# First pair of gate/up blocks: plain products by halves of tokens instead of Strassen's seven, with the sums for later blocks made meanwhile on VectorE

## The chip, the cores and the metric

The kernel runs on one core of a Trainium2 chip. That core has five engines with a queue of instructions each: TensorE (PE, matrix products, with the loading of its stationary operand shown apart as PEld), VectorE (DVE), ScalarE (ACT), GpSimd (POOL) and SyncE (SP, which here issues DMA transfers). They run side by side and wait for one another through semaphores. The metric is the device time of one execution in microseconds. A profile of one execution shows every instruction with start and duration.

## What is computed

One layer of a hybrid network on 640 tokens (512 latent tokens and 128 context tokens) of 2048 features: modulation, a mixing part (a recurrent scan beside a gated unit), an output projection with a residual, and a channel mixer. The part that matters here is the last two steps, from the reference:

```python
    x = x + g1 * (jnp.concatenate([o_a, o_b], axis=-1) @ lp['w_out'])
    h = _rmsnorm(x, lp['norm2_g']) * (1.0 + sc2) + sh2
    ff = (jax.nn.silu(h @ lp['w_ffn_gate']) * (h @ lp['w_ffn_up'])) @ lp['w_ffn_down']
    return x + g2 * ff, s_fin
```

The hidden width of the channel mixer is 5632, that is 44 blocks of 128 columns. Everything is float32.

## The kernel before

**Precision.** TensorE multiplies in a reduced float32 format (`F32R`). Each operand is therefore split into a high part (a cast, on ACT) and a low part (the operand less its high part, on DVE), and a product is the sum of three matmuls: hi x hi, hi x lo, lo x hi. `operand` (L1249) splits a 128x320 piece of the activations, `parts` (L1349) a 128x512 tile of weights (four 128x128 stationary operands). A tile of weights is loaded by one DMA of 256 KB, cast on ACT (L1352), subtracted on DVE (L1353) and used by 12 matmuls of 320 columns.

**Strassen.** The activations stand transposed in 16 tiles `x1T[0..15]` of 128 features x 640 tokens. The tokens fall into two halves, `t1` and `t2`, of 320; the features into two halves of eight tiles (`x1T[j]` and `x1T[j + 8]`). A gate block and the up block of the same columns form the other factor, again two halves of features by two of outputs. A product of 2x2 blocks takes eight block products, or seven in Strassen's way (the Winograd form) with sums on both sides. `seven` (L1408) does one block in seven products in the order `PORD` = 1, 2, 3, 7, 5, 6, 4, each of 24 matmuls: 168 matmuls a block. The sums of the weights are made by `combined` on POOL (L1366), 8 instructions a block. The operands of the activations, `X[i, j]` for product i and feature tile j, are made once and stay in memory for all 44 blocks: 1 and 2 are the plain first token half, 5 starts from the sum of the two feature halves of the second token half, 6, 3 and 7 from differences, 4 is plain.

**The seam.** The output projection (L1295 to L1315) runs in two passes, first for `t1`, then for `t2`, over 16 column tiles. After each pass the sum of squares over the features is complete (`stats`, L1285), and the scale `rs` for that half of the tokens comes from DVE, ACT and DVE (L1291 to L1293). For `t1` the normalized activations (`first_half`) are made during the second pass, and so are operands 1 and 2 for j below 4. Those of `t2` can only begin when the second pass and its statistics are done. `second_half(j)` (L1326) then scales two tiles (one on DVE, one on POOL), applies the modulation on ACT in two pieces, makes Strassen's sums partly on POOL (L1339, L1344), partly on DVE (L1340, L1342), and splits the operands.

`seven_first` (L1368) computes block 0 with all seven products open at once: half of products 1 and 2, then `second_half` for j = 0 to 3, then the first half of the features of the other products, with `second_half` for j = 4 to 7 between them, then the rest.

**What sets the order.** Each engine runs its queue strictly in order. The order within a queue is fixed when the kernel is built: the framework goes by the order in the program, takes the earliest instruction that its own time model says is ready, and adds the waits. A tile can be allocated when the tile that had its tag before is no longer read. What the model has wrong shows on the chip as an engine waiting at the head of its queue with other work behind.

**Later.** A `Gate` object takes the seven sums of a block from the matmul accumulators, forms gate and up, applies SiLU and multiplies (`act`). After each pair of blocks `stores` makes the Strassen sums of `act` for the down projection on POOL and writes them to memory (`d_op`, `d_os`). The down projection (L1733) works in the same way; `load_ops` (L1460) fetches its operands during the last gate/up block into tiles whose tags `stags` lists (then L1481 and L1482 split them), and `load_down` (L1447) its weights into tiles whose tags `wtags` lists. Those tags are places of `x1T`, which hold operands of the gate/up blocks until these end. `ops` and `dloads` are advanced at set products of the last block.

## Time and profile before

| | us |
|---|---|
| median of three runs | 3535.55 |
| lowest and highest | 3533.24, 3540.5 |
| the profiled execution | 3527.76 |
| its span, first to last instruction | 3526.0 |

Busy time in the span: PE 3283.1 us (93%), weight loads 2943.3 (83%), DVE 2523.4 (72%), ACT 1438.5 (41%), POOL 1269.8 (36%). The mean granted clock of TensorE is 0.961 of full speed.

How to read the rows: a row of the timeline gives start and duration in us, engine, line of the kernel, operation, output tile, input tiles and shape; "x2" means that two instructions are merged into the row; in brackets stands how long the engine had been idle and what ended it ("<-ACT hi L1352": the cast of line 1352 on ACT). A row of groups gives the busy time and the mean duration in ns of one instruction, then the idle time before them. A row of stretches gives the busy time of each engine in that stretch, the granted clock, the busy share of the DMA engines, and GB/s. A row "who waited for whom" gives the total wait, how often, and the longest.

### The profile page before, as it was taken

Reading aid. Unit: us, or ns where it says so; the run is one execution under the profiler, and the core shown is the slowest. Engines: PE = TensorE matmul, PEld = TensorE weight load, DVE = VectorE, ACT = ScalarE, POOL = GpSimd, SP = SyncE. Lnnn points to the kernel's source line nnn. Section 1 sums busy time; section 2 is a strip of 40 time slices with the busy share of each in tenths; the row PEclk is TensorE's granted clock in tenths of the full one; section 3 lists DMA queues with packets and bytes.
Section 4 is the critical chain, followed back from the end, with each engine's and each line's share of the span. In section 5 each row is a group of like instructions: output and inputs, shape, how many; then the busy total and the mean of one; then the engine's idle time right before and its main releaser. Section 6 shows DMA issues by size and latency. Waiting matters only on the chain.

```text
span 3526.0 us, 72626 instructions
## 1 busy us (share of the span) xinstructions
PE 3283.1 (93%) x28212; PEld 2943.3 (83%) x28212; DVE 2523.4 (72%) x4524; ACT 1438.5 (41%) x3123; POOL 1269.8 (36%) x1066
## 2 busy tenths in 40 slices
PE   6999989998899999999769999999999999999996
PEld 3687767776777877778769999999999999999986
DVE  4547557756766766654788788888888877877787
ACT  3333334433443433333454444444444444443355
POOL 0001111111111103230356565656565644555533
PEclk8998999998999999998879999999999999999998
DMA  8666666656666767644423434343434345544553
GB/s 315 231 196 169 169 167 181 187 163 154 175 173 174 182 203 230 207 148 137 143 60 111 127 107 123 111 126 107 124 111 125 106 152 162 167 128 123 156 168 111
DMA packets 728049, 546.97 MB, mean 155 GB/s; under 512 B 139496, under 2 KB 661752, under 8 KB 718872
## 3 DMA queue, kind: packets, MB, share of 16 engines
q1 hardware_dynamic: 717176, 528.63, 50.1%
q0 software_dynamic: 8192, 13.13, 2.0%
q8 instruction: 222, 3.64, 0.4%
q14 instruction: 123, 1.01, 0.1%
q10 hardware_dynamic: 2336, 0.57, 0.1%
HBM read 433.53 MB, written 111.28 MB: 155 GB/s over the span
## 4 chain that ended last, share of the span: by engine, by line
PE 39%; DVE 6%; issue 5%; DMA 3%; ACT 1%; POOL 1%; DVEq 0%; SPq 0%; ACTq 0%; POOLq 0%
PE P L1431 13%; PE P L1429 12%; PE P L1430 12%; DVE lo L1353 2%; DMA d_os<-act 2%; DVE act L1554 1%; DMA opd<-d_op 1%; DVE xo L1256 0%; DVE xd L1482 0%; PE big L1306 0%; PE big L1304 0%; PE big L1305 0%; ACT hi L1352 0%; DVE out L1788 0%; POOL rawd L1366 0%
## 5 line engine op out<-in xcount | busy, mean ns | idle before, releaser
L1431 PE MATMUL P<-xo,lo 128*128 128x320 f32 x2408 | 748.5, 311 | 11.4 <-DVE lo L1353 11.4
L1429 PE MATMUL P<-xo,hi 128*128 128x320 f32 x2408 | 746.0, 310 | 2.0 <-ACT hi L1352 1.9
L1430 PE MATMUL P<-xo,hi 128*128 128x320 f32 x2408 | 744.7, 309 | 0.0
L1353 DVE TENSOR_TENSOR lo<-raw,hi 128x512 fp32r<-128x512 f32 x528 | 582.6, 1121 | 72.4 <-ACT hi L1352 67.6
L1352 ACT CAST hi<-raw 128x512 fp32r<-128x512 f32 x528 | 324.5, 622 | 421.7 <-PE P L1430 323.6
L181 PE MATMUL big<-h_hi,hi 128*128 128x320 f32 x1376 | 458.8, 334 | 11.1 <-ACT hi L161 5.5
L1431 PEld LDWEIGHTS P<-xo,lo 128*128 128x128 f32 x2408 | 452.6, 188 | 19.4 <-DVE lo L1353 19.4
L1429 PEld LDWEIGHTS P<-xo,hi 128*128 128x128 f32 x2408 | 452.6, 188 | 4.4 <-ACT hi L1352 4.0
L1430 PEld LDWEIGHTS P<-xo,hi 128*128 128x128 f32 x2408 | 452.7, 188 | 0.0
L183 PE MATMUL big<-h_hi,lo 128*128 128x320 f32 x1376 | 442.7, 323 | 7.6 <-DVE lo L162 7.6
L182 PE MATMUL big<-h_lo,hi 128*128 128x320 f32 x1376 | 443.8, 323 | 0.7 <-DVE h_lo L337 0.7
L1366 POOL TENSOR_TENSOR raw<-raw 128x512 f32<-128x512 f32 x264 | 426.2, 1623 | 16.2 <-DVE lo L1353 5.9
L1431 PE MATMUL P<-xd,lo 128*128 128x320 f32 x1232 | 385.0, 312 | 15.8 <-DVE lo L1353 15.5
L1429 PE MATMUL P<-xd,hi 128*128 128x320 f32 x1232 | 383.0, 311 | 4.6 <-ACT P L1729 2.5
L1430 PE MATMUL P<-xd,hi 128*128 128x320 f32 x1232 | 382.0, 310 | 0.0
L162 DVE TENSOR_TENSOR lo<-raw,hi 128x512 fp32r<-128x512 f32 x268 | 184.9, 694 | 231.2 <-ACT hi L161 219.6
L181 PEld LDWEIGHTS big<-h_hi,hi 128*128 128x128 f32 x1376 | 268.1, 195 | 93.0 <-issue 59.0
L161 ACT CAST hi<-raw 128x512 fp32r<-128x512 f32 x268 | 165.8, 620 | 354.0 <-PE big L182 164.0
L183 PEld LDWEIGHTS big<-h_hi,lo 128*128 128x128 f32 x1376 | 268.0, 195 | 22.0 <-DVE lo L162 10.3
L182 PEld LDWEIGHTS big<-h_lo,hi 128*128 128x128 f32 x1376 | 268.7, 195 | 13.3 <-issue 7.3
L1352 ACT CAST hi<-rawd 128x512 fp32r<-128x512 f32 (+1 forms) x288 | 169.5, 589 | 241.9 <-PE P L1430 206.2
L1431 PEld LDWEIGHTS P<-xd,lo 128*128 128x128 f32 x1232 | 232.5, 189 | 23.0 <-DVE lo L1353 22.8
(358 smaller groups left out, 6287.1 us busy)
## 6 DMA issues: line engine op xcount, KB each, us to landing
wt<-in_w_mod_dram SPq DMA_DIRECT2D x96, 1024.0 KB
rec<-d_S SPq DMA_DIRECT2D x80, 576.0 KB
raw<-in_w_ffn_gate_dram SPq DMA_DIRECT2D x176, 256.0 KB
raw<-in_w_ffn_up_dram SPq DMA_DIRECT2D x176, 256.0 KB
raw<-in_w_in_dram SPq DMA_DIRECT2D x172, 256.0 KB
rawd<-in_w_ffn_down_dram SPq DMA_DIRECT2D x128, 256.0 KB
raw<-in_w_out_dram SPq DMA_DIRECT2D x96, 256.0 KB
xd<-d_os SPq DMA_DIRECT2D x66, 320.0 KB
```

The source lines that it names most:

```text
L161: S.copy(hi, raw)
L162: V.tensor_sub(lo, raw, hi.bitcast(F32))
L181: TE.matmul(halves[hf], hi[:, k, :], h_hi[:, kb, s], start=(kb == 0), stop=False)
L182: TE.matmul(halves[hf], hi[:, k, :], h_lo[:, kb, s], start=False, stop=False)
L183: TE.matmul(halves[hf], lo[:, k, :], h_hi[:, kb, s], start=False, stop=(kb == KB - 1))
L1352: S.copy(hi[:, 0:nk], raw[:, 0:nk])
L1353: V.tensor_sub(lo[:, 0:nk], raw[:, 0:nk], hi[:, 0:nk].bitcast(F32))
L1366: G.tensor_tensor(out=o[:, 0:nk], in0=p[:, 0:nk], in1=q[:, 0:nk], op=ALU.subtract)
L1429: TE.matmul(ps, hi[:, k, :], xk[:, 0, :], start=f, stop=False)
L1430: TE.matmul(ps, hi[:, k, :], xk[:, 1, :], start=False, stop=False)
L1431: TE.matmul(ps, lo[:, k, :], xk[:, 0, :], start=False, stop=l)
L1554: V.tensor_sub(lo, src, hi.bitcast(F32))
```

## The change

Blocks 0 and 1 (f = 0 and its partner, which together form the first pair) are computed by plain products, eight instead of seven per block, and by halves of the tokens. `PLAIN` lists seven entries (block, half of the features, halves of the tokens); an entry takes four tiles of weights. The first four entries need the first token half, the fourth both, the last three the second half alone. The plain operands of the second token half, `X[5, j]` and `X[4, j]`, are made in `second_half`; `sums(j)`, between the later entries, makes Strassen's operands 7, 6 and 3 on DVE, and operand 5 is split a second time at the end, from the sum. `plain_out` forms SiLU(gate) x up from the accumulators. Three tiles of weights are loaded during the last column of the projection, and two of them are split before its last statistic.

```diff
+    JORD = (6, 7, 0, 1, 2, 3, 4, 5)
+    SPARE = ["rs2"] + [f"x1_{m}" for m in (15, 0, 8, 1, 9, 2, 10, 3, 11, 4, 12)]
+
     def operand(i, j, src):
-        if j >= 6 and i != 4:
-            x = xap.tile([P, 2, HALF], F32R, tag=f"x1_{(1, 2, 3, 7, 5, 6).index(i) + 8 * (j - 6)}", name="xo")
+        m = JORD.index(j)
+        if i in (3, 6, 7) and m >= 4:
+            x = xap.tile([P, 2, HALF], F32R, tag=SPARE[3 * (m - 4) + (3, 7, 6).index(i)], name="xo")
         else:
-            x = xpool(i, j).tile([P, 2, HALF], F32R, tag=f"xo{i}_{j}", name="xo")
+            k = m if i in (3, 6, 7) else j
+            x = xpool(i, k).tile([P, 2, HALF], F32R, tag=f"xo{i}_{k}", name="xo")
...
+    PLAIN = ((0, 0, (0,)), (1, 0, (0,)), (0, 1, (0,)), (1, 1, (0, 1)), (0, 1, (1,)), (0, 0, (1,)), (1, 0, (1,)))
+    PW, READY, gus = [], [], []
+    def load_plain():
+        for n, q, _ in PLAIN:
+            for w, k0 in ((w_ffn_gate, 0), (w_ffn_gate, 8), (w_ffn_up, 0), (w_ffn_up, 8)):
+                pool, bufs = (gus[0], RAWB) if gus else (st, 3)
+                raw = pool.tile([P, 4, P], F32, tag="raw", name="raw", bufs=bufs)
+                f, r0 = ORDER[n], (k0 + 4 * q) * P
+                nc.sync.dma_start(raw, w[0, r0:r0 + 512, f * P:f * P + P].rearrange("(k p) n -> p k n", p=P))
+                PW.append(raw)
+                yield
+    first = load_plain()
...
+                if hf and m == KB - 1:
+                    for _ in range(3):
+                        next(first)
                 if sqs:
                     stats()
...
+        for _ in range(2):
+            READY.append(parts(PW.pop(0)))
         stats()
...
     def second_half(j):
-        for kb in (j, j + 8):
+        for kb, i in ((j, 5), (j + 8, 4)):
             x = x1T[kb]
-            (V if kb < 8 else G).tensor_tensor(out=x[:, t2], in0=x[:, t2], in1=rs[:, t2], op=ALU.mult)
+            V.tensor_tensor(out=x[:, t2], in0=x[:, t2], in1=rs[:, t2], op=ALU.mult)
             for (lo, hi, v) in ((HALF, 384, 1), (384, T, 0)):
                 S.activation(x[:, lo:hi], x[:, lo:hi], AF.Identity, scale=modc[4][:, kb, v:v + 1],
                              bias=modc[3][:, kb, v:v + 1])
+            operand(i, j, x[:, t2])
+    def sums(j):
         a11, a21, a12, a22 = x1T[j][:, t1], x1T[j][:, t2], x1T[j + 8][:, t1], x1T[j + 8][:, t2]
-        if j > 3:
-            operand(1, j, a11)
-            operand(2, j, a12)
         s3 = gu.tile([P, HALF], F32, tag="s3", name="s3")
-        G.tensor_tensor(out=s3, in0=a11, in1=a21, op=ALU.subtract)
+        V.tensor_sub(s3, a11, a21)
+        operand(7, j, s3)
         V.tensor_add(a21, a21, a22)
-        operand(5, j, a21)
         V.tensor_sub(a11, a21, a11)
         operand(6, j, a11)
-        G.tensor_tensor(out=a12, in0=a12, in1=a11, op=ALU.subtract)
-        operand(7, j, s3)
-        operand(4, j, a22)
+        V.tensor_sub(a12, a12, a11)
         operand(3, j, a12)
...
-    def seven_first(b11, b12, b21, b22, hook):
...
+    def plain(e):
+        n, q, hs = PLAIN[e]
+        for u in range(2):
+            for b in range(2):
+                hi, lo = READY.pop(0) if READY else parts(PW.pop(0))
+                next(loads, None)
+                for h in hs:
+                    if (n, u, h) not in CP:
+                        CP[n, u, h] = pP.tile([P, 512], F32, tag="P", name="C")[:, 0:HALF]
+                    ps, i = CP[n, u, h], ((1, 2), (5, 4))[h][b]
+                    for k in range(4):
+                        xk = X[i, 4 * q + k]
+                        m = DONE.get((n, u, h), 0)
+                        DONE[n, u, h] = m + 3
+                        TE.matmul(ps, hi[:, k, :], xk[:, 0, :], start=m == 0, stop=False)
+                        TE.matmul(ps, hi[:, k, :], xk[:, 1, :], start=False, stop=False)
+                        TE.matmul(ps, lo[:, k, :], xk[:, 0, :], start=False, stop=m == 45)
+    def plain_out(n, h):
+        if h == 0:
+            acts.append(xap.tile([P, T], F32, tag=f"x1_{6 + n}", name="act"))
+        pa, dst = tmp("pa"), acts[n][:, (t1, t2)[h]]
+        S.activation(pa, CP[n, 0, h], AF.Silu)
+        V.tensor_mul(dst, pa, CP[n, 1, h])
+        if h == 0:
+            nc.sync.dma_start(d_op[0, n], dst)
+    def first_blocks():
+        plain(0)
+        plain(1)
+        for j in range(4, 8):
+            operand(1, j, x1T[j][:, t1])
+            operand(2, j, x1T[j + 8][:, t1])
+        for j in range(4, 8):
+            second_half(j)
+        plain(2)
+        plain(3)
+        for j in range(4):
+            second_half(j)
+        for j in JORD[:2]:
+            sums(j)
+        for n in range(2):
+            plain_out(n, 0)
+        plain(4)
+        plain(5)
+        for j in JORD[2:4]:
+            sums(j)
+        plain(6)
+        for j in JORD[4:]:
+            sums(j)
+        for n in range(2):
+            plain_out(n, 1)
+        for j in JORD:
+            operand(5, j, x1T[j][:, t2])
+        stores(0)
...
-    wtags, stags, ctags = tags(2, 10, 3, 11, 4, 12, 5, 13, 14, 15), tags(0, 8, 1, 9), tags(6, 7, 0, 8)
+    wtags, stags, ctags = tags(13, 2, 11, 10, 4, 3, 12, 5, 14, 15), tags(8, 1, 0, 9), tags(6, 7, 0, 8)
...
-    loads = load_w(0)
-    for _ in loads:
-        pass
-    loads = load_w(1)
-    for _ in range(4):
+    loads = itertools.chain(first, load_w(2), load_w(3))
+    for _ in range(9):
         next(loads)
...
-                self.c = xap.tile([P, 2, HALF], F32, tag=f"x1_{14 + f % 2}", name="c")
+                self.c = xap.tile([P, 2, HALF], F32, tag=f"x1_{(14, 5)[f % 2]}", name="c")
...
-    for f in range(NFF):
+    first_blocks()
+    for f in range(2, NFF):
         b = {n: [WB.pop((f, n, q)) for q in range(2)] for n in ("11", "12", "21", "22")}
         bs = b["11"], b["12"], b["21"], b["22"]
-        for o in seven(*bs, lambda i, k: X[i, k], Gate(f)) if f else seven_first(*bs, Gate(f)):
+        for o in seven(*bs, lambda i, k: X[i, k], Gate(f)):
```

More of the change, by code (lines that the diff above doesn't have):

```diff
@@ L1322, in flow_step @@
     gu = gux.enter_context(tc.tile_pool(name="gu", bufs=2))
+    gus.append(gu)
     xcp = xcx.enter_context(tc.tile_pool(name="xcp", bufs=1, side="right"))
@@ L1366, in combined @@
             G.tensor_tensor(out=o[:, 0:nk], in0=p[:, 0:nk], in1=q[:, 0:nk], op=ALU.subtract)
[L1368 to L1385 removed]
+    CP, DONE = {}, {}
```

43 lines of the change are left out of this document (7 added, 36 removed).

## The prediction

> **What bounds the kernel now.** I read the page first, then the busy table by stretches, to find where TensorE (PE) is not full.
>
> ```profile
> span 3526.0 us, 72626 instructions
> ```
> ```profile
> core 0: us, PE busy (x) PEld busy (x) DVE busy (x) ACT busy (x) POOL busy (x), PEclk, DMA share, GB/s
> ...
> 1742.30:1806.80 64.50, 21.82 (x78) 17.04 (x77) 53.88 (x78) 36.62 (x87) 40.27 (x34) 0.63 0.24 68
> 1822.57:1847.20 24.63, 24.63 (x170) 24.63 (x169) 21.29 (x25) 11.27 (x18) 13.89 (x9) 1.00 0.33 98
> ```
>
> Over the span PE is 93% busy, and the second row (gate/up block 1) shows it full at full clock. The first row is the seam between the output projection and the gate/up blocks: 64.5 us, PE busy in a third of it and at 0.63 of its clock, VectorE (DVE) busy in 53.9 us. The end of the projection in DVE's timeline, PE's timeline after it, and PE's waits from 1742 to 1830:
>
> ```profile
> 1742.33 0.68 DVE L983 SCALAR_TENSOR_TENSOR x1T<-big,modc,x1T 128x64 f32<-128x64 f32 x2 [3.38 <-PE big L1306]
> ```
> ```profile
> 1748.41 0.63 PE L1380 MATMUL P<-xo,hi 128*128 128x320 f32 x1 [3.99 <-ACT hi L1352]
> ...
> 1777.31 0.64 PE L1380 MATMUL P<-xo,hi 128*128 128x320 f32 x1 [20.73 <-ACT hi L1352]
> ...
> 1822.57 0.31 PE L1429 MATMUL P<-xo,hi 128*128 128x320 f32 x1
> ...
> 1823.01 0.31 PE L1429 MATMUL P<-xo,hi 128*128 128x320 f32 x1
> ```
> ```profile
> PE P L1380 <- ACT hi L1352: 29.6, 6, 20.7
> PE P L1382 <- DVE lo L1353: 12.3, 5, 3.9
> ```
>
> The projection's last matmul (L1306) releases DVE at 1742.33. Block 0 (168 matmuls) ends at 1822.57, where L1429, block 1, begins. Three matmuls take 0.44 us there, so one takes 0.147 and a block 24.6; block 2 then begins at 1847.2 and block 3 at 1871.8. From the projection's end to block 2 go 105 us, of which matmuls at full rate need 49.3. The weights' hi and lo, for which PE waits, stand in ACT's and DVE's queues behind the Strassen sums of the activations: that is the 20.7 us gap.
>
> **The change part by part.**
>
> *PE.* Two plain blocks are 7 entries of PLAIN, 28 weight tiles with 384 matmuls where two Strassen blocks have 336: 384 x 0.147 = 56.3 us, 7.0 more than before at full rate. With no stall block 2 would begin at 1742.3 + 56.3 = 1798.6, 48.6 us earlier. What is left is what PE will wait for.
>
> *First weights.* Three tiles are now loaded in the last projection column, into the slots of its own weights, and two of them split ahead of the last statistic.
>
> ```profile
> 1731.45 0.37 SPq L160 DMA_DIRECT2D raw<-in_w_out_dram  x1
> ...
> 1744.80 2.03 SPq L1514 DMA_DIRECT2D raw<-in_w_ffn_gate_dram  x4
> ```
> ```profile
> 1737.06 0.69 DVE L162 TENSOR_TENSOR lo<-raw,hi 128x512 fp32r<-128x512 f32 x1 [1.57 <-ACT hi L161]
> ```
> ```profile
> 1747.74 0.62 ACT L1352 CAST hi<-raw 128x512 fp32r<-128x512 f32 x1 [2.28 <-DMA raw<-in_w_ffn_gate_dram]
> ...
> 1750.15 0.62 ACT L1352 CAST hi<-raw 128x512 fp32r<-128x512 f32 x1 [0.60 <-DMA raw<-in_w_ffn_gate_dram]
> ```
>
> The projection's last load goes out at 1731.5 and its last lo ends at 1737.8, so the third slot is free before 1738 and the three tiles are in by about 1741. They feed 36 matmuls, 5.3 us, to 1747.6. The fourth tile needs memory of the closed pools, as today: issued at 1744.8, landed 1747.7, the next at 1750.1. With hi and lo (0.6 and 0.7) PE waits some 2 us in all; bounds 0 (landing as in the projection) and 5 (every early tile at 2.4 us against PE's 1.76). The 28 tiles against 16 today are 3 MB more, 256 KB for each 1.76 us or more, 149 GB/s at most; SP issues nothing else there but the stores of two halves of act. I put 0 on it later.
>
> *ACT.* `second_half` for j 4 to 7 stands in program order ahead of the weights of the third entry.
>
> ```profile
> 1775.90 0.83 ACT L1255 CAST xo<-x1T 128x320 fp32r<-128x320 f32 x2
> ...
> 1778.57 1.75 ACT L1332 ACTIVATE x1T<-x1T,modc,modc 128x64 f32<-128x64 f32 x4
> ```
>
> A k-block costs ACT two affine pieces (1.75 / 4 each) and a cast (about 0.4): 1.2 us. The statistics end with the reciprocal at 1747.64 (below). Eight k-blocks are 9.7 us, and the hi of the second entry (4 x 0.52) 2.1: ACT is through at about 1760, where PE, having run 96 matmuls (14.1) and waited 2, wants the third entry at 1758.4: 2 us lost. Bounds: 0, and the 20.7 of the same pattern today; I take 2 since neither the sums (L1339 to L1344) nor POOL are in this chain any more. The other eight k-blocks come after the fourth entry, and their weights go first.
>
> *DVE.* It takes over POOL's share (8 scalings, 16 sums) and splits operand 5 twice, which also adds 8 casts to ACT.
>
> ```profile
> 1745.49 2.15 DVE L1293 RECIPROCAL rs<-rs 128x320 f32<-128x320 f32 x1 [0.54 <-ACT rs L1292]
> ...
> 1771.12 0.48 DVE L1340 TENSOR_TENSOR x1T<-x1T 128x320 f32<-128x320 f32 x1
> 1771.52 0.48 DVE L1256 TENSOR_TENSOR xo<-s,xo 128x320 fp32r<-128x320 f32 x1
> ...
> 1823.58 0.68 DVE L1353 TENSOR_TENSOR lo<-raw,hi 128x512 fp32r<-128x512 f32 x1
> 1824.18 0.48 DVE L1589 TENSOR_TENSOR c<-P,pq 128x320 f32<-128x320 f32 x1
> ```
> ```profile
> L1256 DVE TENSOR_TENSOR xo<-x1T,xo 128x320 fp32r<-128x320 f32 x36 | 23.9, 708 | 3.7 <-ACT xo L1255 3.7
> ...
> L1353 DVE TENSOR_TENSOR lo<-raw,hi 128x512 fp32r<-128x512 f32 x18 | 15.2, 857 | 6.1 <-ACT hi L1352 6.0
> L1366 POOL TENSOR_TENSOR raw<-raw 128x512 f32<-128x512 f32 x9 | 12.7, 1413 | 5.5 <-DVE lo L1353 5.3
> ...
> L1330 POOL TENSOR_TENSOR x1T<-x1T,rs 128x320 f32<-128x320 f32 x8 | 8.8, 1133 | 53.4 <-DVE rs L1293 53.4
> L1330 DVE TENSOR_TENSOR x1T<-x1T,rs 128x320 f32<-128x320 f32 x8 | 8.7, 1117 | 0.0
> ```
>
> Undisturbed, a 128x320 step takes 0.40 us (start to start) and a lo 0.60. Beside POOL the same scaling took 1.117: eight on each engine, in the same microseconds. In the new stage POOL has nothing until block 2's weight sums, so I take the undisturbed price. From 1747.64: 32 for `second_half`, 56 for `sums`, 4 for `plain_out`, 8 for the second operand 5, and 4 left of operands 1 and 2: 104 x 0.40 = 41.6. Lo: 25 left of the 28, and 6 that block 2 needs through its third product: 31 x 0.60 = 18.6. Sum 60.2, to 1807.8. Block 2's first four weight sums (4 x 1.4 us on POOL) fall into the end and slow DVE meanwhile, some 3 us; waits for casts another 3: 1814. PE, at 1798.6 + 2 + 2 + 1 (clock, below) = 1803.6, wants the last sums for the second half of product 3, 60 matmuls or 8.8 us later: 1812.4. DVE is 2 late, and I add 2 because block 2's first lo stand behind the sums in program order. Effective start of block 2: 1807.6, so **39.6 us** saved. Below stands 48.6 (no waits); above, DVE at the disturbed price, rival 1.
>
> *New waits.* Operands 3, 6, 7 of the last four j go into old x1T slots; x1_0 to x1_4 are free only when operand 5 was split again, which waits for entry 7 on PE. Queued behind are at most 5 splits of 0.4 us, and PE wants them from 1810 on: inside the 2 above. `plain_out` writes into x1_6 and x1_7, likewise freed by operand 5; all eight PSUM banks are then held, so block 2's second product waits if these are late. The same 2 us.
>
> *The clock.* Where DVE or ACT hold PE up, there is a second price:
>
> ```profile
> 2884.35 0.94 SPq L1474 DMA_DIRECT2D opd<-d_op  x2
> ```
> ```profile
> 2887.76 1.18 ACT L1481 CAST xd<-opd 128x320 fp32r<-128x320 f32 x3 [3.56 <-DMA opd<-d_op]
> ```
> ```profile
> 2889.51 0.41 PE L1429 MATMUL P<-xo,hi 128*128 128x320 f32 x1 [0.55 <-ACT hi L1352]
> ...
> 2892.13 0.42 PE L1431 MATMUL P<-xo,lo 128*128 128x320 f32 x1 [2.06 <-DVE lo L1353]
> ...
> 2893.06 0.47 PE L1430 MATMUL P<-xo,hi 128*128 128x320 f32 x1
> ```
>
> After waits of 0.55 and 2.06, matmuls of 0.47 follow, spaced 0.267, for about 3.3 us: 12 of them, 0.12 too long each, 1.4 us. I put 1 us into the sum for one such fall; bounds 0 and 4. The Trainium skill ("TensorE: Matmul & The Clock Gate", part 1) says the clock is halved only after an idle window of about 3.4 us; by that my stalls of 2 us cost no clock and the sum would be 1 us better; the row above, with 2.06, does not agree with it.
>
> *The seam to the down projection.* The same rows show ACT's queue held 3.6 us by the first operand load (`load_ops`), 2.6 idle on PE and the 1.4 of clock. After the change the four tags of these loads belong to operands 3, 7, 6 and 6 of the last block instead of 1, 1, 2, 2: they come free after its third, fourth and sixth product, not its first and second, and `load(2)` goes out only 3.5 us before the block ends. Bounds: -4 (today's stall goes) and +12 (three such stalls more); I take +2, as the first down product needs only `load(1)`.
>
> Sum: 39.6 - 2 = **38 us**. The profiled execution took 3527.76 (span 3526.0); 3490 on its scale. The median of the three runs is 7.8 higher, 3535.55, and the forecast on that scale is **3497**.
>
> **Rivals.**
>
> 1. *DVE becomes the bound.* For: it is already the busiest here, 53.9 of 64.5 us, and gets more work. At the group means less the 0.08 of overlap: 104 x 0.63 + 31 x 0.78 = 89.7, to 1837.3; product 3's second half and four products follow (15.8): block 3 at 1853.1 against 1871.8, 18.7 less, 17 after the seam: 3519. Against: these means are from beside POOL. The Trainium skill ("Perfetto Trace Analysis", Identifying the Most-Contended Engine) says to relieve the engine with the highest occupancy, judging TensorE by weight loads; here that is DVE (84%) against 17.0 of 64.5 for the loads, so by that rule the change loads the wrong engine.
>
> 2. *The gain is given back at the down projection.* Three stalls at 4 us each: 39.6 - 12 = 28 us, 3508. For: the later slots. Against: 42 blocks lie between, so the order can absorb it.
>
> 3. *The order doesn't do what it says.* The weights still stand behind sums, once before the third entry and once before block 2, 20 us each as in the 20.7 us gap: nothing is left, 3535. Against: the sums are now written behind the weights.
>
> 4. *Slower.* DVE pays beside other engines what the scalings paid: steps of 1.04, for lo too. 135 x 1.04 = 140 us, to 1888, block 3 at 1904: 32 later, 3568. It decides from a mean step of (1871.8 - 15.8 - 1747.6) / 135 = 0.80 us. Against: 0.40 wherever POOL rests.
>
> **How the numbers follow.** Forecast 0.62 (3489 to 3505), rival 1 0.15, rival 2 0.13, rival 3 0.06, rival 4 0.04. The range reaches from no waits at all with today's seam stall gone (48.6 + 4: 3484) to rival 1 (3520) and leaves out rivals 3 and 4. About 0.2%, 7 us, is what a measurement can tell from no change: faster 0.90, same 0.06, slower 0.04.
>
> **What would show it.** Right: matmuls of the first entry follow the projection within 1 us; PE's clock stays near 1.0 up to block 2; DVE's 320-column steps near 0.48 long; block 2 about 62 to 66 us after the projection. Wrong: a PE gap over 5 us before the third entry (ACT) or block 2 (DVE); DVE steps near 0.7; gaps of PE where the first operands of the down projection load, above today's 2.6. If the whole gain shows in the stage and not in the time, it is the seam.

## The result, and the profile after

| | before | after |
|---|---|---|
| median, us (6 runs each) | 3534.39 | 3504.21 |
| lowest and highest | 3519.8, 3540.5 | 3498.36, 3507.59 |
| the profiled execution | 3527.76 | 3498.74 |
| its span | 3526.0 | 3496.9 |

The ratio of the times is 0.9915, with a 95% interval of 0.9894 to 0.9936: 30 us, 0.85%, faster. The forecast was 3497 (3484 to 3520).

The head of the page of the kernel after:

```profile
span 3496.9 us, 72729 instructions
...
PE 3282.1 (94%) x28260; PEld 2946.7 (84%) x28260; DVE 2497.4 (71%) x4544; ACT 1437.1 (41%) x3129; POOL 1223.3 (35%) x1026
```

PE has 48 matmuls more than before and is busy as long. The gain is idle time at the seam, and the busy table of the kernel after shows it. The first row goes from the projection to block 2, the second is block 2:

```profile
core 0: us, PE busy (x) PEld busy (x) DVE busy (x) ACT busy (x) POOL busy (x), PEclk, DMA share, GB/s
1748.73:1812.70 63.97, 58.62 (x389) 56.76 (x388) 59.41 (x119) 47.68 (x106) 8.27 (x4) 1.00 0.54 158
1812.70:1845.80 33.10, 27.62 (x170) 27.10 (x169) 22.65 (x32) 13.37 (x27) 16.34 (x12) 0.90 0.38 114
```

The seam is now full of plain products at full clock, and DVE, busy for 59 of 64 us, holds PE up for only 2.7 us of it. The loss has moved into block 2, which takes 33.1 us instead of 24.6. Who waited for whom on PE, from the projection's end to block 3, in the kernel after:

```profile
PE P L1482 <- ACT hi L1300: 3.3, 1, 3.3
PE C L1416 <- DVE lo L1301: 2.7, 2, 1.9
PE P L1484 <- DVE lo L1301: 2.2, 1, 2.2
PE C L1414 <- ACT hi L1300: 1.4, 1, 1.4
PE ss L1319 <- ACT sq L1346: 0.7, 1, 0.7
PE C L1414 <- DVE rs L1322: 0.6, 1, 0.6
```

Before, the two largest of these rows were 29.6 and 12.3 us.

**Where the 29 us of the two spans lie.** All times below count from the end of the projection, taken as the start of its last matmul plus one spacing (0.15 us): 1742.13 before, 1748.59 after.

| stretch | before | after | gained |
|---|---|---|---|
| start of the span to the projection's end | 1742.13 | 1748.59 | -6.5 |
| from there to block 2 | 105.08 | 64.12 | |
| from there to block 3 | 129.71 | 97.24 | 32.5 |
| block 3 to the first matmul of the down projection | 1035.73 | 1028.83 | 6.9 |
| from there to the end of the span | 618.43 | 622.24 | -3.8 |

Behind the projection's end the gain is 35.6 us (1783.87 against 1748.31). The first row is no work of the change that a trace shows: up to 33 us before the projection's end the order in every engine's queue is the same in both kernels, and 370 us before it the kernel after is 7 us behind already. That end scatters: in the eleven profiles of variants of the changed kernel below, the projection ended between 1739.65 and 1763.26, and in the variant of the old kernel at 1755.90.

**Block 3 to the down projection.** Most of the 6.9 is the stall that the prediction showed in the last gate/up block. From its first matmul to the first of the down projection that block took 29.56 us before and takes 24.64 now. The same place in ACT's timeline of the kernel after:

```profile
2858.92 0.62 ACT L1300 CAST hi<-t 128x512 fp32r<-128x512 f32 x1 [1.18 <-PE P L1483]
2860.63 0.62 ACT L1300 CAST hi<-raw 128x512 fp32r<-128x512 f32 x1 [1.09 <-PE P L1483]
2862.44 0.62 ACT L1300 CAST hi<-raw 128x512 fp32r<-128x512 f32 x1 [1.18 <-PE P L1483]
2864.20 0.82 ACT L1534 CAST xd<-opd 128x320 fp32r<-128x320 f32 x2 [1.15 <-DMA opd<-d_op]
...
2875.65 1.18 ACT L1534 CAST xd<-opd 128x320 fp32r<-128x320 f32 x3 [3.27 <-DMA opd<-d_op]
```

Before, the first cast of a down operand (L1481, now L1534) stood ahead of the hi of both "t" tiles and held them 3.56 us. Now both of these and two "raw" go first, and the DMA wait costs PE nothing. A wait of 3.27 us for a later load has moved into the down projection. From there to the end PE's waits for lo and hi sum to 21.8 us instead of 16.8, and all the waits that the view lists to 23.7 instead of 20.5, most of the 3.8 us of the last row. That row too has a scatter: 619.5 to 624.2 us in the variants of the changed kernel, 620.0 in the variant of the old one.

### The profile page after: what moved, and what is told of

Read it like the earlier page. It is cut to its first block, busy times and chain, and to the rows that moved or that the text cites. A ratio compares the mean times of both kernels' runs of the same rounds, so it can differ in the third digit from the quotient of the medians.

```text
span 3496.9 us, 72729 instructions
## 1 busy us (share of the span) xinstructions
PE 3282.1 (94%) x28260; PEld 2946.7 (84%) x28260; DVE 2497.4 (71%) x4544; ACT 1437.1 (41%) x3129; POOL 1223.3 (35%) x1026
## 4 chain that ended last, share of the span: by engine, by line
PE 40%; DVE 6%; issue 5%; DMA 2%; ACT 1%; POOL 0%; DVEq 0%; ACTq 0%; SPq 0%; POOLq 0%
PE P L1484 13%; PE P L1482 12%; PE P L1483 12%; DVE lo L1301 2%; DMA d_os<-act 1%; DVE act L1603 1%; DMA opd<-d_op 0%; DVE xd L1535 0%; PE big L1337 0%; PE big L1335 0%; PE big L1336 0%; DVE out L1838 0%; ACT hi L1300 0%; PE C L1416 0%; PE C L1414 0%
## 5 line engine op out<-in xcount | busy, mean ns | idle before, releaser
L1484 PE MATMUL P<-xo,lo 128*128 128x320 f32 x2352 | 731.8, 311 | 11.1 <-DVE lo L1301 11.1
L1482 PE MATMUL P<-xo,hi 128*128 128x320 f32 x2352 | 728.6, 310 | 3.7 <-ACT hi L1300 3.6
L1483 PE MATMUL P<-xo,hi 128*128 128x320 f32 x2352 | 727.7, 309 | 0.0
L1484 PEld LDWEIGHTS P<-xo,lo 128*128 128x128 f32 x2352 | 442.3, 188 | 19.3 <-DVE lo L1301 19.2
L1482 PEld LDWEIGHTS P<-xo,hi 128*128 128x128 f32 x2352 | 442.5, 188 | 5.2 <-ACT hi L1300 4.9
L1483 PEld LDWEIGHTS P<-xo,hi 128*128 128x128 f32 x2352 | 442.5, 188 | 0.0
L1395 POOL TENSOR_TENSOR raw<-raw 128x512 f32<-128x512 f32 x252 | 408.7, 1631 | 11.6 <-DVE lo L1301 1.5
L1395 POOL TENSOR_TENSOR t<-raw 128x512 f32<-128x512 f32 x84 | 136.0, 1619 | 345.0 <-DMA raw<-in_w_ffn_up_dram 338.4
```

What stands on the lines that cost most here:

```text
L1395: G.tensor_tensor(out=o[:, 0:nk], in0=p[:, 0:nk], in1=q[:, 0:nk], op=ALU.subtract)
L1482: TE.matmul(ps, hi[:, k, :], xk[:, 0, :], start=f, stop=False)
L1483: TE.matmul(ps, hi[:, k, :], xk[:, 1, :], start=False, stop=False)
L1484: TE.matmul(ps, lo[:, k, :], xk[:, 0, :], start=False, stop=l)
```

## The experiments

Each kernel was profiled once. Block starts and the stretch from the projection's end to the end of the span ("rest") come from that profile, and the ratio from runs of the kernel before on the same chip. The medians come from several chips and are not to be compared with one another. a_oldtags, a_bank and a_st have the order of the kernel after in every queue from the projection's end to block 3, so these four rows show the scatter of one profile: 64.0 to 65.7 for block 2, 96.2 to 97.5 for block 3.

| run | block 2 | block 3 | rest | median | ratio, interval |
|---|---|---|---|---|---|
| before | 105.1 | 129.7 | 1783.9 | 3534.39 | |
| b_vector | 96.1 | 120.7 | 1775.9 | 3523.43 | 0.9965 (0.9945 to 0.9984) |
| a_pool | 80.2 | 108.8 | 1758.9 | 3512.82 | 0.9922 (0.9899 to 0.9945) |
| after | 64.1 | 97.2 | 1748.3 | 3504.21 | 0.9915 (0.9894 to 0.9936) |
| a_oldtags | 64.0 | 96.2 | 1748.8 | 3502.76 | 0.9906 (0.9876 to 0.9937) |
| a_nopre | 67.7 | 100.0 | 1753.1 | 3498.83 | 0.9889 (0.9863 to 0.9915) |
| a_dve2 | 63.5 | 97.5 | 1749.9 | 3499.59 | 0.9905 (0.9886 to 0.9924) |
| a_pa2 | 65.6 | 99.6 | 1753.0 | 3497.73 | 0.9899 (0.9873 to 0.9925) |
| a_bank | 65.6 | 97.5 | 1748.7 | 3502.78 | 0.9902 (0.9881 to 0.9924) |
| a_pa2dve2 | 61.8 | 95.9 | 1748.7 | 3499.83 | 0.9899 (0.9885 to 0.9914) |
| a_st | 65.7 | 97.3 | 1751.7 | 3501.23 | 0.9902 (0.9886 to 0.9919) |
| a_op5 | 65.6 | 95.3 | 1749.5 | 3510.77 | 0.9923 (0.9902 to 0.9945) |
| a_best | 63.2 | 95.7 | 1746.1 | 3495.06 | 0.9880 (0.9860 to 0.9900) |
| a_nopool | 63.4 | 88.2 | 1740.0 | 3492.77 | 0.9888 (0.9868 to 0.9908) |

The times tell the variants of the changed kernel apart only where they differ by more than about 10 us. The block starts carry the rest of the argument.

### Order or engine?

The change does two things: it puts plain products ahead of the sums, and it moves POOL's share of the sums and scalings to VectorE. Two runs do one without the other. "Order" stands here for all of the change but the engine, the early weights and the tags included; Strassen's seven products written ahead of the sums were not tried. First the old order with POOL's share on VectorE (b_vector):

```diff
-            (V if kb < 8 else G).tensor_tensor(out=x[:, t2], in0=x[:, t2], in1=rs[:, t2], op=ALU.mult)
+            V.tensor_tensor(out=x[:, t2], in0=x[:, t2], in1=rs[:, t2], op=ALU.mult)
-        G.tensor_tensor(out=s3, in0=a11, in1=a21, op=ALU.subtract)
+        V.tensor_sub(s3, a11, a21)
-        G.tensor_tensor(out=a12, in0=a12, in1=a11, op=ALU.subtract)
+        V.tensor_sub(a12, a12, a11)
```

> The kernel before, with POOL's eight scalings and sixteen sums of the seam put on VectorE, and the order left as it is. Two theories of where the gain comes from. Order theory: PE waits because the weights' casts stand behind the Strassen sums, so from the projection's end to block 2 (105.0 us before) it stays at 97 to 103 us (DVE loses about 16 us of disturbed durations and gets 24 x 0.40 = 9.6 more), and the time moves by less than 8 us. Contention theory: DVE was slow because POOL worked beside it, so the stretch falls to about 75 us and the time to about 3505.

Then the changed kernel with that share given back to POOL (a_pool), the same three lines the other way round.

> The changed kernel, with half of the scalings and the sums s3 and a12 given back to POOL as before. From the projection's end to block 3 it was 96.5 us in the changed kernel, 129.5 before. Order theory: most of the gain stays, 97 to 108 us, since DVE has 24 steps less but the rest dearer. Contention theory: DVE's 320-column steps go back to a mean of 0.7 us or more, and the stretch to 120 us or more.

The engine alone brings block 3 from 129.7 to 120.7, 9.0 us; the order alone to 108.8, 20.9 us; both together 32.5. Most is order, and with the old order the old wait stays. Neither theory met its numbers: the order theory came near (block 2 at 96.1 where it had 97 to 103, 12 us of time where it had under 8; block 3 at 108.8 where it had 97 to 108), and the contention theory missed by 21 us in b_vector and 11 in a_pool. PE's waits from the projection's end to block 3 in b_vector:

```profile
PE P L1380 <- ACT hi L1352: 22.2, 5, 10.8
PE P L1382 <- DVE lo L1353: 10.0, 4, 5.1
```

The engine is worth 9.0 us in the old order and 11.6 in the new one, although VectorE gets more work by it. The groups by line for DVE and POOL show why, from the projection's end to block 3, first in a_pool, then in the kernel after:

```profile
L1301 DVE TENSOR_TENSOR lo<-raw,hi 128x512 fp32r<-128x512 f32 x39 | 36.1, 933 | 13.5 <-ACT hi L1300 13.5
L1262 DVE TENSOR_TENSOR xo<-x1T,xo 128x320 fp32r<-128x320 f32 x40 | 25.0, 650 | 3.3 <-ACT xo L1261 3.3
L1367 DVE TENSOR_TENSOR x1T<-x1T,rs 128x320 f32<-128x320 f32 x8 | 7.0, 904 | 0.0
...
L1367 POOL TENSOR_TENSOR x1T<-x1T,rs 128x320 f32<-128x320 f32 x8 | 8.8, 1138 | 53.4 <-DVE rs L1324 53.4
```
```profile
L1301 DVE TENSOR_TENSOR lo<-raw,hi 128x512 fp32r<-128x512 f32 x39 | 30.2, 785 | 8.3 <-ACT hi L1300 8.3
L1262 DVE TENSOR_TENSOR xo<-x1T,xo 128x320 fp32r<-128x320 f32 x40 | 20.7, 539 | 1.1 <-ACT xo L1261 1.1
L1367 DVE TENSOR_TENSOR x1T<-x1T,rs 128x320 f32<-128x320 f32 x16 | 7.1, 484 | 0.0
```

Sixteen scalings on VectorE take 7.1 us. Eight on VectorE beside eight on POOL take 7.0 on VectorE and 8.8 on POOL: POOL's help frees no time. Meanwhile it lengthens VectorE's lo (933 against 785 ns) and operand steps (650 against 539).

### The tags and the early weights

The new tag lists for the down projection were priced at 2 us. In a_oldtags they are the old ones:

```diff
-    wtags, stags, ctags = tags(13, 2, 11, 10, 4, 3, 12, 5, 14, 15), tags(8, 1, 0, 9), tags(6, 7, 0, 8)
+    wtags, stags, ctags = tags(2, 10, 3, 11, 4, 12, 5, 13, 14, 15), tags(0, 8, 1, 9), tags(6, 7, 0, 8)
```

> The changed kernel, with the lists of tags of the down projection's loads as before (0, 8, 1, 9 and 2, 10, 3, 11, ...). If the tags matter at this seam, the first operand load now waits for x1_0, which holds an operand 6 of the last block, until its sixth product: the first down product then waits some 3 us for load and split, with 1.4 us of halved clock, so 3 to 6 us more from block 3 to the end. If the loads are hidden anyway, the first down matmul follows the last gate/up matmul without a gap, as in the changed kernel, and nothing changes. In both cases everything up to block 3 is as in the changed kernel.

Block 3 to the first down matmul took 1030.0 us (after 1028.8), and the down projection and what follows 622.6 (after 622.2). The 4.9 us are not back with the old list, but part of them is: the last gate/up block takes 26.6 us instead of 24.6, and the first down matmul waits 1.82 us for its operand's cast, less than the first theory's 3 to 6. In the sum of both stretches the lists differ by 1.6 us, which one profile of each does not show. In both runs the hi of the "t" tiles stand ahead of the down operands in ACT's queue, as shown above; that this order removed the stall, and which of the change's lines turned it, was not tried.

In a_nopre the three early tiles of weights are left out, and all weights are loaded behind the projection:

```diff
-                if hf and m == KB - 1:
-                    for _ in range(3):
-                        next(first)
...
-        for _ in range(2):
-            READY.append(parts(PW.pop(0)))
...
-    for _ in range(9):
+    for _ in range(12):
         next(loads)
```

> The changed kernel without the three early weight tiles: the first twelve are loaded when the pools are open, as before. If PE's start sets the end of the stage, the first plain matmul comes 5 to 6 us after the projection (2.7 in the changed kernel), and block 3 comes 3 to 5 us later (96.5 us after the projection's end in the changed kernel, here 100 to 102). If DVE's sum of work sets it, block 3 comes within 1 us of 96.5, since DVE's work begins with the statistics either way.

The first plain matmul came 6.26 us after the projection instead of 2.83, and block 3 2.8 us later, near the first theory's 3 to 5. That does not show that PE's start binds, for VectorE ran later too: it had two more lo parts to make behind the projection and stood 0.73, 0.94 and 1.13 us for their hi. Against PE's start speak a_bank and a_st, where a fall of the clock let PE begin block 2 some 1.5 us later than in the kernel after, and block 3 came at most 0.3 us later. The times cannot show 3 us.

### What holds block 2?

Block 2 stands 3.28 and 2.20 us, and then pays for the clock. PE's timeline there, in the kernel after:

```profile
1816.44 0.41 PE L1482 MATMUL P<-xo,hi 128*128 128x320 f32 x1 [3.28 <-ACT hi L1300]
...
1819.19 0.63 PE L1484 MATMUL P<-xo,lo 128*128 128x320 f32 x1 [2.20 <-DVE lo L1301]
1819.62 0.47 PE L1482 MATMUL P<-xo,hi 128*128 128x320 f32 x1
1819.89 0.47 PE L1483 MATMUL P<-xo,hi 128*128 128x320 f32 x1
```

Twenty matmuls follow one another at 0.267 us instead of 0.147: 2.4 us. Three causes offered themselves. POOL makes block 2's first four weight sums shortly before, and VectorE's steps beside them are long (S1). DVE's and POOL's timelines, in the kernel after:

```profile
1802.00 0.48 DVE L1379 TENSOR_TENSOR x1T<-x1T 128x320 f32<-128x320 f32 x1
1802.41 1.77 DVE L1301 TENSOR_TENSOR lo<-raw,hi 128x512 fp32r<-128x512 f32 x1
1804.11 1.58 DVE L1382 TENSOR_TENSOR x1T<-x1T 128x320 f32<-128x320 f32 x1
1805.62 1.59 DVE L1380 TENSOR_TENSOR x1T<-x1T 128x320 f32<-128x320 f32 x1
1807.13 1.55 DVE L1262 TENSOR_TENSOR xo<-x1T,xo 128x320 fp32r<-128x320 f32 x1
...
1815.82 2.05 DVE L1262 TENSOR_TENSOR xo<-x1T,xo 128x320 fp32r<-128x320 f32 x2
1817.79 1.34 DVE L1301 TENSOR_TENSOR lo<-raw,hi 128x512 fp32r<-128x512 f32 x1
```
```profile
1799.90 3.74 POOL L1395 TENSOR_TENSOR t<-raw 128x512 f32<-128x512 f32 x1 [98.16 <-DMA raw<-in_w_ffn_up_dram]
1803.72 1.63 POOL L1395 TENSOR_TENSOR raw<-raw 128x512 f32<-128x512 f32 x1
1805.31 1.55 POOL L1395 TENSOR_TENSOR t<-raw 128x512 f32<-128x512 f32 x1
1806.94 1.40 POOL L1395 TENSOR_TENSOR raw<-raw 128x512 f32<-128x512 f32 x1
1815.58 0.87 POOL L1582 TENSOR_TENSOR s<-act 128x320 f32<-128x320 f32 x1 [7.25 <-DVE xo L1262]
1816.53 0.99 POOL L1584 TENSOR_TENSOR act<-act 128x320 f32<-128x320 f32 x1
```

Or ACT's queue is held by a Silu that waits for its one buffer (S2), in ACT's timeline:

```profile
1809.71 0.44 ACT L1423 ACTIVATE pa<-C 128x320 f32<-128x320 f32 x1 [3.81 <-DVE act L1424]
```

Or it is what stands ahead in VectorE's queue: eight subtractions for the fifth product (S3a), or the stretch beside POOL's four stores of the first pair, from 1815.58 on (S3b).

a_dve2 makes the four weight sums on VectorE:

```diff
-        combine(t3, b22, b12)
-        combine(b12, b12, b11)
+        combined(t3, b22, b12, nk, eng)
+        combined(b12, b12, b11, nk, eng)
...
-        for o in seven(*bs, lambda i, k: X[i, k], Gate(f)):
+        for o in seven(*bs, lambda i, k: X[i, k], Gate(f), eng=V if f == 2 else G):
```

> The changed kernel with the first four weight sums of block 2 (the t3 and b12 of its first half) made by VectorE instead of POOL. In the profile after, block 2 starts 64.1 us after the projection's end and block 3 at 97.2, 33.1 instead of some 24.6 us later; PE stands 3.28 and 2.20 us inside it. Theory S1 (these four POOL sums, at 1799.9 to 1808.3, lengthen VectorE's steps beside them to 1.5 to 1.8 us instead of 0.48 to 0.68): the sums cost VectorE about 4 x 0.5 us, and the steps beside them lose some 4 to 5 us: block 3 starts 91 to 94.5 us after the projection's end. Theory S2 (ACT's queue is held 3.8 us by the second Silu of the plain products, which waits for its one buffer pa): block 3 stays at 96 to 99. Time: 3 us or less off, within the interval.

a_pa2 gives the second Silu a buffer of its own, and a_pa2dve2 is both edits:

```diff
-        pa, dst = tmp("pa"), acts[n][:, (t1, t2)[h]]
+        pa, dst = tmp(("pa", "pq")[n]), acts[n][:, (t1, t2)[h]]
```

> The changed kernel with a buffer of its own for the second Silu of the plain products, so that it need not wait for VectorE's multiplication of the first. Theory S2 (ACT's queue is held 3.81 us at 1809.71 by that Silu, and the hi parts that block 2 waits for, 3.28 us, stand behind it): the hi wait in block 2 falls below 1 us and block 3 starts 91 to 94.5 us after the projection's end. Theory S1 (VectorE beside POOL is what is late; ACT's hi parts only follow VectorE's differences): block 3 stays at 95.5 to 99, with the wait named after VectorE or moved to the lo parts.

> Both: the second Silu with its own buffer and block 2's first four weight sums on VectorE. If S1 alone holds, block 3 starts as in the run with the four sums moved (within 1 us); if S2 alone, as in the run with the second buffer; if each holds a part, the gains add up and block 3 starts 88 to 92 us after the projection's end; if neither, 96 to 99 in all of them and VectorE's sheer sum of steps is the bound (59.4 of 64 us busy).

Neither theory held. Block 3 came at 97.5, 99.6 and 95.9. In a_dve2 the hi wait fell to 1.36 and the lo wait grew to 5.94. In a_pa2 the hi wait stayed at 3.00 and the lo wait grew to 3.71. In a_pa2dve2 the Silu no longer waits, the hi wait is down to 1.04 and the long steps at the four sums are gone, but PE stands 6.11 us for one lo. VectorE's queue ahead of that lo, in a_pa2dve2:

```profile
1808.34 3.96 DVE L1262 TENSOR_TENSOR xo<-x1T,xo 128x320 fp32r<-128x320 f32 x4
...
1812.63 1.28 DVE L1395 TENSOR_TENSOR t<-raw 128x512 f32<-128x512 f32 x2
1813.84 1.28 DVE L1395 TENSOR_TENSOR raw<-raw 128x512 f32<-128x512 f32 x2
1815.04 1.88 DVE L1301 TENSOR_TENSOR lo<-raw,hi 128x512 fp32r<-128x512 f32 x3
```

Four subtractions at 1.0 us stand beside POOL's stores (1807.8 to 1812.0), and then the four sums that had just been moved to VectorE.

a_bank exchanges the two accumulator pools of the projection, for the 0.58 us before the first plain matmul:

```diff
-        pss = ph.enter_context(tc.tile_pool(name="pss", bufs=1, space=PSUM))
         pb2 = ph.enter_context(tc.tile_pool(name="pb2", bufs=2, space=PSUM))
+        pss = ph.enter_context(tc.tile_pool(name="pss", bufs=1, space=PSUM))
```

> The changed kernel with its two accumulator pools exchanged, so that the first plain product's accumulator is not the bank from which VectorE and ACT read the projection's statistic. Theory: the first plain matmul waits for that bank (0.58 us before it, named after the statistic's rs); then it comes 2.2 us or less after the projection's end instead of 2.83, and block 3 some 0.6 us earlier. Rival: the rs itself (the operand's scale) is what it waits for; then nothing moves (2.8 us, block 3 at 96.5 to 98). No difference of the times to be told.

Nothing moved: 2.82 us, and the same 0.58 named after rs. Another placement of the accumulators was not tried.

The next runs took S3. a_st calls the first pair's stores behind block 2's third product; a_op5 makes the eight operands of the fifth product during block 2's first two:

```diff
@@ a_st
-        stores(0)
...
+                if f == 2:
+                    stores(0)
@@ a_op5
-        for j in JORD:
-            operand(5, j, x1T[j][:, t2])
...
+            if f == 2 and o < 2:
+                for j in JORD[4 * o:4 * o + 4]:
+                    operand(5, j, x1T[j][:, t2])
```

> The changed kernel with the first pair's stores (the four POOL operations on act, s3) moved behind the third product of block 2, VectorE's order unchanged. Behind block 2's start, at 1815.6 to 1819.9 of the profile after, these four POOL operations lie beside VectorE's last operand subtractions, of which each takes about 1.0 there instead of 0.40, and the lo parts 1.2 instead of 0.6. Theory S3b (this stretch is what makes block 2's parts late): VectorE has them 3 us earlier, and block 3 starts 92 to 95 us after the projection's end instead of 97.2. Theory S3a (they are late because 8 subtractions for the fifth product stand ahead of them in VectorE's queue): 95 to 98.

> The changed kernel with the eight operands of the fifth product (cast on ACT, subtraction on VectorE), which no earlier product reads, made during block 2's first two products instead of ahead of block 2; stores unmoved. VectorE's order then has block 2's lo parts between them. Theory S3a: the parts come 8 x 0.40 = 3.2 us and the stretch beside the stores earlier, PE's two gaps (3.28 and 2.20 us) fall to 2 us or less together and the slow matmuls behind them go: block 3 starts 90 to 93.5 us after the projection's end. Theory S3b: 95 to 98. Rival to both: the operands 7, 6 and 3, whose last subtractions come as late, are what block 2 waits for: the wait is then named after xo and block 3 stays at 95 or more.

a_st tests nothing: the lines moved in the program, but POOL's queue came out in the same order as in the kernel after, so that the run is a repeat of it (block 3 at 97.3 against 97.2, although block 2 came 1.6 later; rest 1751.7 against 1748.3, which shows the scatter of that column). S3b stays untested by it. In a_op5 VectorE's order did change. The two large gaps went, and three of 0.59, 1.97 and 1.54 us came later in the block: block 3 at 95.3, 1.9 us earlier and 0.9 below the scatter of the order after, but outside S3a's 90 to 93.5 and just inside S3b's 95 to 98.

a_best holds all four edits.

> All together: the fifth product's operands and the first pair's stores moved into block 2, block 2's first four weight sums on VectorE, and a second buffer for Silu. If what lies ahead of block 2's parts on VectorE is the cause, block 2's gaps go below 1.5 us in all and block 3 starts 88 to 91.5 us after the projection's end, 6 to 9 us sooner than after: some 3490 to 3499, 0.2% under the changed kernel, and a profiled end minus first down matmul of 622 as in the others. If the stall only moves on (to the operands of products 2, 3 or 7, or to the lo parts of the first products), block 3 stays at 94 or more and the time cannot be told from that of the changed kernel.

Block 3 at 95.7: the stall had only moved on again, to 4.13 us for an operand. VectorE's timeline at that place, in a_best:

```profile
1823.97 1.79 DVE L1301 TENSOR_TENSOR lo<-raw,hi 128x512 fp32r<-128x512 f32 x1
1825.69 7.33 DVE L1262 TENSOR_TENSOR xo<-x1T,xo 128x320 fp32r<-128x320 f32 x6
```

Six subtractions took 1.22 us each, beside eight POOL operations from 1822.4 to 1832.7. Each arrangement had let POOL meet other steps of VectorE. Theory S4 follows: what counts is that POOL runs at all while VectorE is late. a_nopool moves POOL's remaining work up to block 4 to VectorE, 12 weight sums and 4 stores:

```diff
-                combine(b22, b22, b12)
-                combine(b21, b21, b22)
+                combined(b22, b22, b12, nk, eng)
+                combined(b21, b21, b22, nk, eng)
...
+        E = V if p == 0 else G
-        G.tensor_tensor(out=s3, in0=a11, in1=a21, op=ALU.subtract)
+        E.tensor_tensor(out=s3, in0=a11, in1=a21, op=ALU.subtract)
...
-        for o in seven(*bs, lambda i, k: X[i, k], Gate(f), eng=V if f == 2 else G):
+        for o in seven(*bs, lambda i, k: X[i, k], Gate(f), eng=V if f in (2, 3) else G):
```

> The run with all four edits together, and besides all of POOL's work of this stretch on VectorE: block 2's last four weight sums, block 3's eight and the first pair's four stores. VectorE's order up to block 2's parts is that of the run with the four edits; POOL has nothing to do until block 4's sums. In that run six operand subtractions took 7.33 us (1.22 each) and two lo parts 1.8 us beside POOL's sums and stores, and PE stood 4.13 and 1.03 us behind them. Theory S4 (any POOL tensor operation lengthens VectorE's steps beside it two- to fourfold, and every arrangement so far only chose which steps that hits): now all steps up to block 3 keep 0.40 and 0.60 us apart, PE's gaps in block 2 sum to under 1.5 us, no matmul there is slow, and block 3 starts 87 to 90.5 us after the projection's end. Rival: VectorE's sheer count of steps is the bound: the 12 further sums at 0.6 and 4 stores at 0.4 (8.8 us) push the parts later, and block 3 starts at 94 or more. Time by S4: 5 to 8 us below that of the run with the four edits, some 3488 to 3495.

S4 holds, and its rival, VectorE's count of steps, falls. VectorE's order up to these parts is that of a_best, and the same steps, in its timeline in a_nopool:

```profile
1807.32 0.68 DVE L1301 TENSOR_TENSOR lo<-raw,hi 128x512 fp32r<-128x512 f32 x1
1807.92 2.50 DVE L1262 TENSOR_TENSOR xo<-x1T,xo 128x320 fp32r<-128x320 f32 x6
```

The six take 2.50 us instead of 7.33, with more work on VectorE, not less. The busy table of a_nopool, to block 2 and through it:

```profile
1739.80:1803.00 63.20, 59.83 (x389) 58.28 (x388) 57.33 (x121) 48.89 (x108) 0.00 (x0) 0.97 0.57 165
1803.00:1827.90 24.90, 24.90 (x171) 24.68 (x170) 23.06 (x47) 13.00 (x27) 0.00 (x0) 1.00 0.48 147
```

Block 2 runs without a gap at full clock, and block 3 starts at 88.2, 7.5 us sooner than in a_best and 9.0 sooner than in the kernel after. At the end of the span 8.4 are left (rest 1740.0 against 1748.3): 3.4 went on the way to the down projection and 2.8 came behind it, both at the edge of the variants' scatter. The times do not show the step from a_best: 5 to 8 us were expected, and the ratios are 0.9888 and, for a_best, 0.9880. The interval (0.9868 to 0.9908) also overlaps that of the kernel after (0.9894 to 0.9936), and these were timed against separate runs of the kernel before. The gain over the kernel before is shown, 1.1%. Over the changed kernel it is likely and not shown by the times.

## Why the prediction was right, and where not

The mechanism was right: the sums left the path, plain products filled the seam, and block 2 came 64.1 us after the projection (62 to 66 forecast), at a clock of 1.00 and with VectorE's steps near 0.48. By its terms:

| term | forecast, us | measured, us |
|---|---|---|
| before the first plain matmul | 2 | 2.83 |
| third entry, ACT then DVE | 2 | 2.1 |
| last entry, DVE | 0 | 1.9 |
| clock up to block 2 | 1 | 0 |
| what remains up to block 2 | 0 | 1.0 |
| block 2, waits and its own clock | 4 | 8.5 |
| sum of the losses to block 3 | 9 | 16.3 |
| gained to block 3 | 39.6 | 32.5 |
| seam to the down projection | -2 | +1.1 |
| other blocks | 0 | +2.0 |
| behind the projection's end | 38 | 35.6 |

The measured losses are what block 3's start of 97.24 leaves over 56.3 of plain products and 24.64 of block 2. They came out 7.3 us larger than forecast, and 5.1 came back in the seam and the other blocks, which the sum had at -2 and 0. That 35.6 lies so near 38 is in part luck: block 3 to the down projection took 1028.3 to 1032.2 us in the variants, which is as much scatter as the 2.0.

- **The clock up to block 2.** No matmul ran at half rate there in the kernel after. In seven of the nine variants with the same early weights and VectorE's sums, 12 or 13 did, 1.5 us, behind the waits of the third or the last entry. So the forecast of one such fall was well sized, and the clock of 1.00 was luck of one execution.
- **First weights.** The wait was sought in the fourth tile's DMA, and there was none. PE stood 0.73 us for the last statistic's squares, and 0.58 in a wait named after its result, instead. The size was near, the cause wrong, and "within 1 us of the projection" was wrong.
- **ACT ahead of the third entry.** 1.35 us for a hi and then 0.75 for a lo: the size as forecast, a third of it VectorE's.
- **VectorE's price.** The undisturbed 0.40 held until POOL began. This step is the one that decided against rival 1, and a_pool comes near rival 1's price and its block 3 (108.8 against 111) where POOL does work beside it.
- **Block 2.** This is the term that was mis-sized. The prediction gave "some 3 us" to POOL's four weight sums. They cost VectorE 4.4 (four steps took 6.2 us from start to start instead of 1.8), and the first pair's four stores, which it did not price beside VectorE, cost 2.5 more (the next steps took 4.3 us from start to start instead of 1.8). To these 6.9 comes the clock: 2.4 us for a fall that the sum had at 1 in all. The split is read from the trace: no run takes POOL alone out of the changed kernel's own order, and a_dve2, which took out the four sums, only moved the wait. a_nopool, with the edits of a_best besides, loses 0.2 us in block 2, where the sum had 4. It starts block 3 at 88.2, near the 89.9 of the prediction's own sum, but by chance, for it loses 7.1 up to block 2, where the sum had 5.
- **The seam to the down projection.** Later slots were to cost 2 us. They cost nothing: it is with the old list (a_oldtags) that the first down matmul waits 1.82 us. The stall of the last gate/up block went (4.9 us) and 3.8 came back later, so rival 2 did not occur: the value lies within the bounds of -4 and +12, and the one taken had the wrong sign.
- **The two medians.** 35.6 behind the projection became 29.1 in the two spans, since the projection ended 6.5 us later in the execution profiled after, and 30.2 in the medians. With ends of the projection from 1740 to 1763 in the variants, whether the change itself moves that end on average is not settled by one profile of each.

The Trainium skill ("Perfetto Trace Analysis", Identifying the Most-Contended Engine), by whose rule the prediction had the change load the wrong engine, does not agree with these runs: b_vector gave the busiest engine more work and gained 9 us of stage. Part of that engine's busy time was the lengthening beside POOL, 1117 ns for a scaling that takes 484 without it. The clock rule of the Trainium skill ("TensorE: Matmul & The Clock Gate", part 1) speaks of an idle window of about 3.4 us; in block 2, 3.28 us of idle followed by 2.20 cost the clock. The ends of matmuls are modelled, so that 3.28 is not surely below 3.4, but much shorter waits cost the clock elsewhere, and not each time: the 1.94 us of the last plain entry cost none in the kernel after, and soon behind the same wait in a_st twelve matmuls run at 0.267. What decides is not shown. PE's timeline there, in the kernel after, then in a_st:

```profile
1809.34 0.42 PE L1416 MATMUL C<-xo,lo 128*128 128x320 f32 x1 [1.94 <-DVE lo L1301]
```
```profile
1807.10 0.42 PE L1416 MATMUL C<-xo,lo 128*128 128x320 f32 x1 [1.94 <-DVE lo L1301]
...
1808.97 0.47 PE L1415 MATMUL C<-xo,hi 128*128 128x320 f32 x1
```

## What to carry to other kernels

Read the price of a step on VectorE together with what POOL does in the same microseconds: helping a late VectorE with tensor operations on POOL (float32 with two inputs in SBUF here) can make it later, and taking POOL's work back can be the cheaper way. When removing a wait only moves it, look for what all arrangements have in common before rearranging again. Put work whose operands are complete ahead of the sums in each queue, and price every engine's next task at the new meeting point, the stores of the finished pair included.

## What the runs showed of the hardware

VectorE's steps with two inputs in the main on-chip memory (SBUF) and POOL's hold one another up, and where POOL's follow closely they take turns, one for one. In the timelines above, VectorE's steps at 1804.11, 1805.62 and 1807.13 are 1.51 apart, and POOL's sums at 1803.72, 1805.31 and 1806.94 are 1.59 and 1.63 apart, where 0.40 is VectorE's own pace. They do not always take turns: during POOL's first sum, from 1799.90, five of VectorE's steps (the last at 1802.00) started 0.40 or 0.60 apart, and it was POOL's sum that took 3.74 us. The Trainium skill ("SBUF — State Buffer", Terms) says that the two engines share a pair of ports that one holds for a whole instruction while the other is blocked; and "GPSIMD Engine Reference", section 1, puts this down to VectorE instructions with two inputs in that memory, among others. The rows agree that one blocks the other; what decides which of them waits they do not show. An operation with one input in the accumulator memory kept its 0.49 us in the middle of POOL's four sums of 2855.06 to 2861.5 (DVE's timeline, and POOL's, of the kernel after). In a_nopre another such kept 0.47 us at 1809.94, inside one POOL sum and between two steps of 1.78 and 1.17:

```profile
2856.01 0.90 DVE L1301 TENSOR_TENSOR lo<-raw,hi 128x512 fp32r<-128x512 f32 x1 [1.02 <-ACT hi L1300]
2857.26 0.49 DVE L1624 TENSOR_TENSOR c<-P,pa 128x320 f32<-128x320 f32 x1 [0.35 <-PE P L1484]
2857.77 0.85 DVE L1301 TENSOR_TENSOR lo<-t,hi 128x512 fp32r<-128x512 f32 x1
```
```profile
2855.06 6.41 POOL L1395 TENSOR_TENSOR raw<-raw 128x512 f32<-128x512 f32 x4 [0.89 <-DVE lo L1301]
```

The other surprise is the scatter of the stretch ahead of the projection's end: 23.6 us between the profiles of a_op5 (1763.26) and a_nopool (1739.65), whose queues have the same order up to there. That is more than most of the effects tried here. The busy tables of that stretch show where it lies: PE is busy for 1619.0 us in a_op5 at a granted clock of 0.93, and for 1595.1 in a_nopool at 0.95. These are 23.9 us apart, as the ends are, while PE's idle time is the same (144.2 and 144.6). So between these two it is the time at half clock that differs (246 us and 178, from the granted clock), not the waits; what makes the clock fall more often was not followed up.
